# A gated recurrence by products of gates that double with each level, in a two-layer decoder trunk

## The chip, the cores and the metric

The kernel runs on one core of a Trainium2 chip. The metric is the device time of one execution in microseconds (us). The kernel before takes 1434.04 us, the median of three runs (1431.91 to 1434.69). The core has five engines with a queue each, which work in order: TensorE (PE, with its weight loads as PEld), VectorE (DVE), ScalarE (ACT), GpSimd (POOL) and SyncE (SP), which issues the transfers.

## The reference

Two decoder layers on 512 tokens of width 1024. In each, one projection feeds three token mixers side by side, whose outputs are concatenated and projected; then a squared-ReLU feed-forward. The change touches the first mixer (four heads of 64 channels):

```
f = lb + (1.0 - lb) * sigmoid(z);  log_f = log(maximum(f, F_MIN));  k = (1.0 - lb) * sigmoid(-z)
bc = cumsum(log_f)                      # within a chunk
decay[t, s] = exp(bc[t] - bc[s])        # for s <= t, else 0
attn[t, s] = sum_k q[t, k] * decay[t, s, k] * k[s, k]
o = attn @ v + (q * exp(bc)) @ state
state = exp(b_last) * state + (k * exp(b_last - bc))^T @ v
```

The decay depends on the channel, so `attn` is not a single product of two matrices.

## The kernel before, in words

All matrices of the projections are held as a high and a low part, and each product is three matmuls (`mm3`). The tile names in the profile: `whi`, `wlo` are the parts of a weight block `wraw`, `hT` the parts of the transposed activations, `acc` the accumulators; `qrope`, `krope` the queries and keys of the second mixer with RoPE (`ropet` is a scratch tile of it, `qs` the query split in two parts), `aps` its scores; `adaw`, `adaq`, `adacc`, `adas`, `grow` belong to the modulation by `c`; `ang`, `kk`, `rr`, `sin2`, `cos2` to the sine and cosine of the positions, which are computed once, in layer 0.

**The recurrence** works on chunks of 128 tokens, with channels on partitions (two tiles `pr` of 128 channels, that is two heads each, by 512 tokens). `hgq` is the query, `hgk` the key factor, `hgs` the sigmoid of the gate. The generator `recurrence()` forms the gate `ft`, its logarithm `lf` (as a sum of two logarithms, so that very small gates keep their value) and the running sum `hb` by a scan on DVE. The 128x128 triangle of `attn` (`hatt`, one tile per chunk, four heads side by side) is then filled by level. Level `lv` pairs blocks of `h_ = 2**lv` tokens: the later block's queries with the earlier block's keys. With the running sum at the boundary as `mid`, `hx` holds `exp(hb - mid)` in the later half of each pair and `exp(mid - hb)` in the earlier half; the first times `hgq` goes into `hbd`, a block-diagonal tile in which the two heads stand apart, the second times `hgk` stays in `hx`, and one matmul per chunk and `pr` gives the level's scores. A predicated copy by a mask (`lmask`, one plane per level, made at the start) writes them into `hatt`. The diagonal comes first: a product of query and key, summed over channels by matmuls with `heads`, evicted as `hdd`, and spread on `ident`. The levels then run from 6 down to 0. At the end of the mixer `hqe` and `hke` (query and key with their decay over the chunk) and `hebl` carry the state `hst` from chunk to chunk.

**The order** is not the program's own. Every call (`V.`, `A.`, `G.`, `PE.`, `SP.`) is recorded as an operation with its dependences; `vg` and `gv` record two alternatives, DVE or POOL, and `copy` ACT or DVE. A planner, `Plan.schedule`, then places all operations of both layers engine by engine, by rules for cost and by the place in the program, several rounds, and keeps the round that it reckons shortest. So an edit in one place can move instructions anywhere. The recurrence advances one step at each `next(rec, None)`, beside every second step of the projections (`beside`).

Of the kernel before, what the change touches and what calls it, by code (L numbers as in the profile page):

```python
# [684 lines left out]
def trunk(ctx: ExitStack, tc: tile.TileContext, I, out, depth=L):  # L685
# [102 lines left out]
    lmask = static([128, 8, 128], U8, "lmask")  # L788
# [4 lines left out]
    for lv in range(7):  # L793
# [8 lines left out]
    V.tensor_copy(lmask[:, 7, :], ident)  # L802
# [361 lines left out]
    def layer(l, yn, xd, sb1, rest, mods):  # L1164
# [77 lines left out]
        hb = [big(name="hb") for _ in range(2)]  # L1242
        hk = hgk
        one_b = ones[:, 0:1].to_broadcast([128, 128])
        TINY = 2.0 ** -60
# [4 lines left out]
        def recurrence():  # L1250
            for pr in range(2):
                ft, lf = big(name="ft"), big(name="lf")
                V.tensor_scalar(ft, hgs[pr], oml[:, l, pr:pr + 1], lb[:, l, pr:pr + 1], op0=OP.mult, op1=OP.add)
                V.tensor_scalar(hk[pr], hgk[pr], oml[:, l, pr:pr + 1], None, op0=OP.mult)
                V.tensor_scalar(lf, ft, TINY, None, op0=OP.max)
                V.tensor_scalar(ft, ft, 1e-30, 2.0 ** 60, op0=OP.max, op1=OP.mult)
                V.tensor_scalar(ft, ft, 1.0, None, op0=OP.min)
                A.activation(lf, lf, AF.Ln)
                A.activation(ft, ft, AF.Ln)
                vg("tensor_add", lf, lf, ft)  # L1260
                for ch in range(NT):
                    sl = slice(ch * 128, (ch + 1) * 128)
                    V.tensor_tensor_scan(hb[pr][:, sl], one_b, lf[:, sl], 0.0, op0=OP.mult, op1=OP.add)
                yield
# [4 lines left out]
            for lv in (7, 6, 5, 4, 3, 2, 1, 0):  # L1269
                if lv == 7:  # L1270
                    p = ps()[:, :16]
                    for pr in range(2):
                        xd_ = big(name="hx")
                        gv("tensor_mul", xd_, hk[pr], hgq[pr])
                        for ch in range(NT):
                            PE.matmul(p[:, ch * 4 + 2 * pr:ch * 4 + 2 * pr + 2], xd_[:, ch * 128:(ch + 1) * 128], heads,
                                      start=True, stop=True)
                    dd = small([128, 16], "hdd", 2)
                    V.tensor_copy(dd, p)
                    for ch in range(NT):  # L1280
                        gv("tensor_mul", atts[ch], ident[:, None, :].to_broadcast([128, 4, 128]),
                           dd[:, ch * 4:ch * 4 + 4][:, :, None].to_broadcast([128, 4, 128]))
                    yield
                    continue
                h_ = 1 << lv
                nb = 512 // (2 * h_)
                vw = "p (n r h) -> p n r h"
                xf = [None, None]
                for pr in range(2):
                    xf[pr] = big(name="hx")  # L1290
                    bd = diag[lv % 2][pr]
                    bv = hb[pr].rearrange(vw, r=2, h=h_)
                    ev = xf[pr].rearrange(vw, r=2, h=h_)
                    mid = bv[:, :, 0, h_ - 1:h_].to_broadcast([128, nb, h_])
                    vg("tensor_sub", ev[:, :, 1, :], bv[:, :, 1, :], mid)
                    vg("tensor_sub", ev[:, :, 0, :], mid, bv[:, :, 0, :])
                    A.activation(xf[pr], xf[pr], AF.Exp)
                    e5 = xf[pr].rearrange("p (c n r h) -> p c n r h", c=NT, r=2, h=h_)
                    q5 = hgq[pr].rearrange("p (c n r h) -> p c n r h", c=NT, r=2, h=h_)
                    for hh in range(2):  # L1300
                        r_ = slice(hh * 64, hh * 64 + 64)
# [676 lines left out]
```

## Time and profile before

| | before |
|---|---|
| median of 3 runs | 1434.04 us |
| the profiled execution | 1432.88 us |
| its span | 1430.6 us |
| PE busy | 1361.7 us (95%) |
| DVE busy | 1097.3 us (77%) |
| ACT busy | 575.5 us (40%) |
| POOL busy | 489.7 us (34%) |

The span runs from the first to the last instruction on the core; the 2.3 us around it belong to the execution's time. Shares are means over stages that differ: the mixer of layer 0 lies at about 36 to 336 us, the feed-forward of layer 0 to about 748, the mixer of layer 1 at about 752 to 1010, and the rest is the feed-forward of layer 1. A busy PE is not PE at its peak, since matmuls overlap and can run at a lower clock.

### The profile page before, as it was taken

Reading aid. Unit: us, or ns where it says so; the run is one execution under the profiler, and the core shown is the slowest. Engines: PE = TensorE matmul, PEld = TensorE weight load, DVE = VectorE, ACT = ScalarE, POOL = GpSimd, SP = SyncE. Lnnn points to the kernel's source line nnn. Section 1 sums busy time; section 2 is a strip of 40 time slices with the busy share of each in tenths; the row PEclk is TensorE's granted clock in tenths of the full one; section 3 lists DMA queues with packets and bytes.
Section 4 is the critical chain, followed back from the end, with each engine's and each line's share of the span. In section 5 each row is a group of like instructions: output and inputs, shape, how many; then the busy total and the mean of one; then the engine's idle time right before and its main releaser. Section 6 shows DMA issues by size and latency. Waiting matters only on the chain.

```text
span 1430.6 us, 21317 instructions
## 1 busy us (share of the span) xinstructions
PE 1361.7 (95%) x7339; PEld 1135.3 (79%) x7339; DVE 1097.3 (77%) x2305; ACT 575.5 (40%) x1517; POOL 489.7 (34%) x687
## 2 busy tenths in 40 slices
PE   5978999989999999999999989999999999999997
PEld 4766788868888888888889787888888888888886
DVE  8998899988976488385788978899895467634567
ACT  6645387872341223212324455887333112210121
POOL 5678735573310000010223876445721000000023
PEclk9988999998999999999999999999999999999998
DMA  9731554225376276284502334112553234423331
GB/s 305 236 92 29 166 173 146 69 90 163 111 228 212 74 236 204 75 293 155 165 13 83 76 115 145 38 45 89 159 158 103 89 103 139 153 62 104 125 110 59
DMA packets 119843, 185.66 MB, mean 130 GB/s; under 512 B 9796, under 2 KB 47160, under 8 KB 119736
## 3 DMA queue, kind: packets, MB, share of 16 engines
q1 hardware_dynamic: 119736, 184.31, 40.6%
q8 instruction: 58, 0.95, 0.3%
q14 instruction: 49, 0.40, 0.1%
HBM read 175.89 MB, written 8.39 MB: 129 GB/s over the span
## 4 chain that ended last, share of the span: by engine, by line
PE 71%; DVE 16%; ACT 5%; POOL 3%; DMA 2%; issue 2%; SPq 1%; POOLq 0%; DVEq 0%; ACTq 0%
PE acc L681 60%; PE aps L681 6%; PE ps L681 5%; DMA adaq<-in_w_ada_dram 2%; DVE adacc L681 2%; ACT P L681 1%; DVE amax L681 1%; ACT KV L681 1%; DVE PT L681 1%; DVE wlo L681 1%; DVE pcT L681 1%; DVE hb L681 1%; DVE hatt L681 1%; DVE hx L681 1%; DVE rt L681 1%
## 5 line engine op out<-in xcount | busy, mean ns | idle before, releaser
L681 PE MATMUL acc<-hT,whi 128*128 128x512 f32 (+1 forms) x1296 | 413.3, 373 | 4.1 <-ACT hT L681 3.8
L681 POOL TENSOR_TENSOR wlo<-wraw,whi 128x256 fp32r<-128x256 f32 (+2 forms) x122 | 134.9, 1114 | 557.2 <-ACT whi L681 425.4
L681 PE MATMUL acc<-whi,aT 128*128 128x512 f32 x896 | 325.2, 394 | 0.0
L681 PEld LDWEIGHTS acc<-hT,whi 128*128 128x128 f32 x1296 | 234.9, 189 | 49.4 <-ACT hT L681 4.5
L681 PE MATMUL acc<-hT,wlo 128*128 128x512 f32 (+1 forms) x648 | 238.6, 371 | 0.3 <-DVE wlo L681 0.3
L681 PE MATMUL acc<-whi,hT 128*128 128x256 f32 (+2 forms) x1024 | 227.1, 307 | 1.5 <-ACT KV L681 0.9
L681 DVE TENSOR_TENSOR wlo<-wraw,whi 128x512 fp32r<-128x512 f32 (+1 forms) x278 | 193.7, 713 | 11.2 <-ACT whi L681 4.7
L681 PEld LDWEIGHTS acc<-whi,aT 128*128 128x128 f32 x896 | 168.2, 188 | 39.5
L681 ACT ACTIVATE whi<-wraw 128x512 fp32r<-128x512 f32 (+2 forms) x262 | 134.6, 554 | 136.9 <-DMA wraw<-in_w_ff_dram 87.2
L681 ACT ACTIVATE ffa<-acc 128x512 f32<-128x512 f32 x64 | 38.2, 597 | 374.4 <-PE acc L681 373.8
L681 PE MATMUL acc<-wlo,aT 128*128 128x512 f32 x448 | 176.6, 394 | 0.0
L681 PEld LDWEIGHTS acc<-whi,hT 128*128 128x128 f32 x1024 | 168.2, 191 | 8.8 <-issue 1.4
L681 PE MATMUL acc<-wlo,hT 128*128 128x256 f32 (+2 forms) x512 | 157.3, 308 | 0.4 <-DVE wlo L681 0.4
L681 DVE TENSOR_TENSOR ffs<-ffa 128x512 f32<-128x512 f32 x64 | 46.4, 727 | 144.4 <-ACT ffa L681 144.2
L681 PEld LDWEIGHTS acc<-hT,wlo 128*128 128x128 f32 x648 | 122.5, 189 | 23.0 <-DVE wlo L681 0.7
L681 DVE SCALAR_TENSOR_TENSOR adacc<-adaw,silc,adacc 128x512 f32<-128x512 f32 x140 | 110.3, 797 | 12.3 <-DMA adaw<-in_w_ada_dram 10.8
L681 PEld LDWEIGHTS acc<-wlo,hT 128*128 128x128 f32 x512 | 97.6, 191 | 3.4 <-DVE wlo L681 0.6
L681 PEld LDWEIGHTS acc<-wlo,aT 128*128 128x128 f32 x448 | 84.2, 188 | 19.7
L681 ACT ACTIVATE P<-aps,amax 128x128 f32<-128x128 f32 (+3 forms) x128 | 67.8, 535 | 18.0 <-DVE amax L681 16.1
L681 DVE TENSOR_REDUCE amax<-aps 128x1 f32<-128x32 f32 (+4 forms) x192 | 65.6, 380 | 6.1 <-PE aps L681 5.1
L681 POOL TENSOR_SCALAR P<-P,acoef 128x256 f32<-128x256 f32 (+3 forms) x76 | 42.9, 579 | 46.5 <-DVE acoef L681 43.0
L681 DVE CAST whi<-wraw 128x512 fp32r<-128x512 f32 (+1 forms) x138 | 57.0, 415 | 0.3 <-issue 0.2
(327 smaller groups left out, 2453.8 us busy)
## 6 DMA issues: line engine op xcount, KB each, us to landing
wraw<-in_w_ff_dram SPq DMA_DIRECT2D x128, 512.0 KB, 4.6
adaw<-in_w_ada_dram SPq DMA_DIRECT2D x80, 512.0 KB, 4.7
wraw<-in_w_in_dram SPq DMA_DIRECT2D x49, 256.0 KB, 3.6
adaq<-in_w_ada_dram SPq DMA_DIRECT2D x32, 256.0 KB, 6.0
wraw<-in_w_o_dram SPq DMA_DIRECT2D x16, 512.0 KB, 3.8
wraw<-in_w_in_dram SPq DMA_DIRECT2D x15, 512.0 KB, 3.9
xd<-xs SPq DMA_DIRECT2D x24, 256.0 KB, 4.1
xr<-xd SPq DMA_DIRECT2D x24, 256.0 KB, 5.0
```

The costliest lines, as they stand in the source:

```text
L681: getattr(self.handles[e], method)(*a, **k)
```

## The change

The logarithm, the scan, the differences and the exponentials go. `f0` is the gate itself, held at 1e-30 or above. `fts[pr][lv]` holds for each block of `2**lv` tokens the product of its gates; the next level's is the product of neighbours, so it has half as many elements. `fq` and `fk` are the tiles `hgq` and `hgk`, now updated in place: at level `lv` the query has the product of the gates from its block's start to itself, the key the product from behind itself to its block's end. So the later block's queries are only copied into `hbd` (by `copy`, ACT or DVE) and the key tile is the matmul's other operand as it stands. After the copy, the queries of later blocks are multiplied by the earlier block's product; after the matmuls, the keys of earlier blocks by the later block's product. The levels run from 0 up to 6, and after level 6 `fq` and `fk` are what `hqe` and `hke` were, and `fts[pr][7]` replaces `hebl`. The diagonal is spread by ACT in 16 pieces of 128x128 per layer, and levels 5 and 6 are evicted by plain ACT copies of rectangles, so the mask has five planes.

```diff
--- before.py
+++ after.py
@@ -785,12 +785,12 @@
     G.iota(ti, pattern=[[1, 128]], base=0, channel_multiplier=0)
     si = static([128, 1], I32, "si")
     G.iota(si, pattern=[[1, 1]], base=0, channel_multiplier=1)
-    lmask = static([128, 8, 128], U8, "lmask")
+    lmask = static([128, 5, 128], U8, "lmask")
     tsh = big((128, 128), I32, name="tsh")
     tsf = big((128, 128), name="tsf")
     s1 = static([128, 4], I32, "s1")
     sf = static([128, 2], F32, "sf")
-    for lv in range(7):
+    for lv in range(5):
         V.tensor_scalar(tsh, ti, lv, None, op0=OP.logical_shift_right)
         V.tensor_copy(tsf, tsh)
         V.tensor_scalar(s1[:, 0:1], si, lv, None, op0=OP.logical_shift_right)
@@ -799,7 +799,6 @@
         V.scalar_tensor_tensor(sf[:, 0:1], sf[:, 1:2], 1000.0, sf[:, 0:1], op0=OP.mult, op1=OP.add)
         V.tensor_scalar(sf[:, 0:1], sf[:, 0:1], 1.0, None, op0=OP.add)
         V.tensor_scalar(lmask[:, lv, :], tsf, sf[:, 0:1], None, op0=OP.is_equal)
-    V.tensor_copy(lmask[:, 7, :], ident)
...
     inv = static([128, 32], F32, "inv")
@@ -1239,82 +1238,82 @@
...
-        hb = [big(name="hb") for _ in range(2)]
-        hk = hgk
-        one_b = ones[:, 0:1].to_broadcast([128, 128])
-        TINY = 2.0 ** -60
+
+
+
+        fq, fk = hgq, hgk
+        F_MIN = 1e-30
+        fts = [[f] for f in hgs]
+        for f in fts:
+            t, at = big(name="hft"), 0
+            for lv in range(1, 8):
+                f.append(t[:, at:at + (512 >> lv)])
+                at += 512 >> lv
...
         atts = [big((128, 4, 128), name="hatt") for _ in range(NT)]
 
         def recurrence():
+            p = ps()[:, :16]
             for pr in range(2):
-                ft, lf = big(name="ft"), big(name="lf")
-                V.tensor_scalar(ft, hgs[pr], oml[:, l, pr:pr + 1], lb[:, l, pr:pr + 1], op0=OP.mult, op1=OP.add)
-                V.tensor_scalar(hk[pr], hgk[pr], oml[:, l, pr:pr + 1], None, op0=OP.mult)
-                V.tensor_scalar(lf, ft, TINY, None, op0=OP.max)
-                V.tensor_scalar(ft, ft, 1e-30, 2.0 ** 60, op0=OP.max, op1=OP.mult)
-                V.tensor_scalar(ft, ft, 1.0, None, op0=OP.min)
-                A.activation(lf, lf, AF.Ln)
-                A.activation(ft, ft, AF.Ln)
-                vg("tensor_add", lf, lf, ft)
+                f0 = fts[pr][0]
+                V.tensor_scalar(f0, hgs[pr], oml[:, l, pr:pr + 1], lb[:, l, pr:pr + 1], op0=OP.mult, op1=OP.add)
+                V.tensor_scalar(fk[pr], hgk[pr], oml[:, l, pr:pr + 1], None, op0=OP.mult)
+                V.tensor_scalar(f0, f0, F_MIN, None, op0=OP.max)
+                xd_ = big(name="hx")
+                vg("tensor_mul", xd_, fk[pr], fq[pr])
                 for ch in range(NT):
-                    sl = slice(ch * 128, (ch + 1) * 128)
-                    V.tensor_tensor_scan(hb[pr][:, sl], one_b, lf[:, sl], 0.0, op0=OP.mult, op1=OP.add)
+                    PE.matmul(p[:, ch * 4 + 2 * pr:ch * 4 + 2 * pr + 2], xd_[:, ch * 128:(ch + 1) * 128], heads,
+                              start=True, stop=True)
+                vg("tensor_mul", fq[pr], fq[pr], f0)
                 yield
             diag = [[big((128, NT, 2, 64), name="hbd") for _ in range(2)] for _ in range(2)]
             for t in diag[0] + diag[1]:
                 for hh in range(2):
                     G.memset(t[hh * 64:hh * 64 + 64, :, 1 - hh, :], 0.0)
-            for lv in (7, 6, 5, 4, 3, 2, 1, 0):
-                if lv == 7:
-                    p = ps()[:, :16]
-                    for pr in range(2):
-                        xd_ = big(name="hx")
-                        gv("tensor_mul", xd_, hk[pr], hgq[pr])
-                        for ch in range(NT):
-                            PE.matmul(p[:, ch * 4 + 2 * pr:ch * 4 + 2 * pr + 2], xd_[:, ch * 128:(ch + 1) * 128], heads,
-                                      start=True, stop=True)
-                    dd = small([128, 16], "hdd", 2)
-                    V.tensor_copy(dd, p)
-                    for ch in range(NT):
-                        gv("tensor_mul", atts[ch], ident[:, None, :].to_broadcast([128, 4, 128]),
-                           dd[:, ch * 4:ch * 4 + 4][:, :, None].to_broadcast([128, 4, 128]))
-                    yield
-                    continue
+            dd = small([128, 16], "hdd", 2)
+            V.tensor_copy(dd, p)
+            for ch in range(NT):
+                for a in range(4):
+                    A.activation(atts[ch][:, a], ident, AF.Copy, scale=dd[:, ch * 4 + a:ch * 4 + a + 1])
+            yield
+            for lv in range(7):
                 h_ = 1 << lv
-                nb = 512 // (2 * h_)
                 vw = "p (n r h) -> p n r h"
-                xf = [None, None]
                 for pr in range(2):
-                    xf[pr] = big(name="hx")
                     bd = diag[lv % 2][pr]
-                    bv = hb[pr].rearrange(vw, r=2, h=h_)
-                    ev = xf[pr].rearrange(vw, r=2, h=h_)
-                    mid = bv[:, :, 0, h_ - 1:h_].to_broadcast([128, nb, h_])
-                    vg("tensor_sub", ev[:, :, 1, :], bv[:, :, 1, :], mid)
-                    vg("tensor_sub", ev[:, :, 0, :], mid, bv[:, :, 0, :])
-                    A.activation(xf[pr], xf[pr], AF.Exp)
-                    e5 = xf[pr].rearrange("p (c n r h) -> p c n r h", c=NT, r=2, h=h_)
-                    q5 = hgq[pr].rearrange("p (c n r h) -> p c n r h", c=NT, r=2, h=h_)
+                    q5 = fq[pr].rearrange("p (c n r h) -> p c n r h", c=NT, r=2, h=h_)
                     for hh in range(2):
                         r_ = slice(hh * 64, hh * 64 + 64)
-                        vg("tensor_mul", bd[r_, :, hh, :].rearrange("p c (n h) -> p c n h", h=h_), e5[r_, :, :, 1, :],
-                           q5[r_, :, :, 1, :])
-                    vg("tensor_mul", ev[:, :, 0, :], ev[:, :, 0, :], hk[pr].rearrange(vw, r=2, h=h_)[:, :, 0, :])
+                        copy(bd[r_, :, hh, :].rearrange("p c (n h) -> p c n h", h=h_), q5[r_, :, :, 1, :])
+                    tv = fts[pr][lv].rearrange("p (n r) -> p n r", r=2)
+                    qv = fq[pr].rearrange(vw, r=2, h=h_)[:, :, 1, :]
+                    nb = 512 // (2 * h_)
+                    vg("tensor_mul", qv, qv, tv[:, :, 0:1].to_broadcast([128, nb, h_]))
+                    vg("tensor_mul", fts[pr][lv + 1], tv[:, :, 0], tv[:, :, 1])
                 for cp_ in range(2):
                     p = ps().rearrange("p (c m) -> p c m", c=2)
                     for c2 in range(2):
                         ch = 2 * cp_ + c2
                         for pr in range(2):
-                            PE.matmul(p[:, c2, pr * 128:(pr + 1) * 128], xf[pr][:, ch * 128:(ch + 1) * 128],
+                            PE.matmul(p[:, c2, pr * 128:(pr + 1) * 128], fk[pr][:, ch * 128:(ch + 1) * 128],
                                       diag[lv % 2][pr][:, ch].rearrange("p a t -> p (a t)"), start=True, stop=True)
                     for c2 in range(2):
+                        att = atts[2 * cp_ + c2].rearrange("p a (n r h) -> p a n r h", r=2, h=h_)[:, :, :, 1, :]
+                        new = p[:, c2].rearrange("p (a n h) -> p a n h", a=4, h=h_)
+                        if h_ >= 32:
+                            for n in range(64 // h_):
+                                r_ = slice(2 * n * h_, (2 * n + 1) * h_)
+                                A.activation(att[r_, :, n], new[r_, :, n], AF.Copy)
+                            continue
                         V.copy_predicated(
-                            atts[2 * cp_ + c2].rearrange("p a (n r h) -> p a n r h", r=2, h=h_)[:, :, :, 1, :],
-                            lmask[:, lv, :].rearrange("p (n r h) -> p n r h", r=2, h=h_)[:, None, :, 1, :]
-                            .to_broadcast([128, 4, 64 // h_, h_]),
-                            p[:, c2].rearrange("p (a n h) -> p a n h", a=4, h=h_))
+                            att, lmask[:, lv, :].rearrange("p (n r h) -> p n r h", r=2, h=h_)[:, None, :, 1, :]
+                            .to_broadcast([128, 4, 64 // h_, h_]), new)
+                for pr in range(2):
+                    tv = fts[pr][lv].rearrange("p (n r) -> p n r", r=2)
+                    kv = fk[pr].rearrange(vw, r=2, h=h_)[:, :, 0, :]
+                    nb = 512 // (2 * h_)
+                    vg("tensor_mul", kv, kv, tv[:, :, 1:2].to_broadcast([128, nb, h_]))
                 yield
 
         rec = recurrence()
@@ -1627,18 +1626,7 @@
         run(filler)
...
-        qe = [big(name="hqe") for _ in range(2)]
-        ke = [big(name="hke") for _ in range(2)]
-        ebl = small([128, 2, 4], "hebl", 2)
-        for pr in range(2):
-            A.activation(qe[pr], hb[pr], AF.Exp)
-            vg("tensor_mul", qe[pr], qe[pr], hgq[pr])
-            b4 = hb[pr].rearrange("p (n t) -> p n t", t=128)
-            k4 = ke[pr].rearrange("p (n t) -> p n t", t=128)
-            vg("tensor_sub", k4, b4[:, :, 127:128].to_broadcast([128, 4, 128]), b4)
-            A.activation(ke[pr], ke[pr], AF.Exp)
-            vg("tensor_mul", ke[pr], ke[pr], hk[pr])
-            A.activation(ebl[:, pr], b4[:, :, 127], AF.Exp)
+        qe, ke = fq, fk
         for k in range(2):
             mixT[k] = pair(name="mixT")
         st_t = [small([128, 2, 128], "hst", 2) for _ in range(2)]
@@ -1674,7 +1662,7 @@
                         if ch == 0:
                             V.tensor_copy(stn[r_, pr, r_], src)
                         else:
-                            V.scalar_tensor_tensor(stn[r_, pr, r_], sprev[r_, pr, r_], ebl[r_, pr, ch:ch + 1],
+                            V.scalar_tensor_tensor(stn[r_, pr, r_], sprev[r_, pr, r_], fts[pr][7][r_, ch:ch + 1],
                                                    src, op0=OP.mult, op1=OP.add)
             sq = big((128, 256), name="hsq")
             A.activation(sq, po[:, :256], AF.Square)
```

Where the instructions now stand, at three places in layer 0.

PE, before, at the recurrence's first matmuls (`heads` sums the diagonal, `hbd,hx` are levels, `ident,qrope` the transposes of the RoPE queries):

```order
L681 MATMUL acc_1189<-wlo_1178,hT_741 128x512
L681 MATMUL acc_1189<-whi_1169,hT_771 128x512
L681 MATMUL ps_1326<-heads,hx_1225 128x2 x4
L681 MATMUL ps_1326<-heads,hx_1273 128x2 x4
L681 MATMUL ps_1340<-hbd_859,hx_1201 128x128
L681 MATMUL ps_1340<-hbd_862,hx_1216 128x128
L681 MATMUL ps_1348<-ident,qrope_1320 128x128 x2
L681 MATMUL ps_1355<-ident,qrope_1324 128x128 x2
```

PE, now, at level 0:

```order
L681 MATMUL acc_870<-wlo_1032,hT_727 128x256
L681 MATMUL ps_1095<-hbd_848,hgk_975 128x128
L681 MATMUL ps_1095<-hbd_845,hgk_955 128x128
L681 MATMUL ps_1095<-hbd_848,hgk_975 128x128
L681 MATMUL ps_1097<-hbd_848,hgk_975 128x128
L681 MATMUL ps_1097<-hbd_845,hgk_955 128x128
L681 MATMUL ps_1097<-hbd_848,hgk_975 128x128
L681 MATMUL acc_870<-whi_1010,hT_757 128x256
L681 MATMUL acc_882<-whi_1004,hT_716 128x256
```

The first products stood behind 131,596 columns of matmuls, `heads` with them, and beside the RoPE transposes; `heads` now stands behind 83,468 and level 0 behind 91,724, amid the projection, and the first RoPE transpose behind 132,684 instead of 131,916.

DVE, before, between the scans and the sine (`hb` are scans):

```order
L681 TENSOR_TENSOR wlo_1174<-wraw_1068,whi_1163 128x512
L681 SCALAR_TENSOR_TENSOR hb_1153<-ones,lf_1064 128x128
L681 SCALAR_TENSOR_TENSOR rr_1033<-kk_934,rr_1033 128x128
L681 SCALAR_TENSOR_TENSOR hb_1195<-ones,lf_1071 128x128 x4
L681 TENSOR_SCALAR hgk_989<-hgk_989,oml 128x512
L681 SCALAR_TENSOR_TENSOR rr_1033<-kk_934,rr_1033 128x128
L681 TENSOR_SCALAR adacc_1232<-adaw_852,silc 128x512
L681 TENSOR_SCALAR kk_934<-ang_703 128x128
```

DVE, now, before the sine:

```order
L681 COPY_PREDICATED hatt_1158<-lmask,ps_1174 128x128x2
L681 TENSOR_TENSOR hgk_975<-hgk_975,hft_1113 128x128x2
L681 TENSOR_TENSOR wlo_1234<-wraw_1045,whi_1197 128x512
L681 COPY_PREDICATED hatt_1048<-lmask,ps_1229 128x64x4
L681 COPY_PREDICATED hatt_1083<-lmask,ps_1229 128x64x4
L681 COPY_PREDICATED hatt_1141<-lmask,ps_1239 128x64x4
L681 COPY_PREDICATED hatt_1158<-lmask,ps_1239 128x64x4
L681 TENSOR_SCALAR kk_920<-kk_920 128x128
L681 SCALAR_TENSOR_TENSOR rr_1269<-kk_920,ang_695 128x128
```

The scans before the sine are gone, and the predicated copies of levels 0 to 2 (twelve) now stand before it.

ACT, now, at the block copies of levels 0 and 1 (`hbd_845` and `hbd_848` are level 0, `hbd_851` level 1):

```order
L681 ACTIVATE hatt_1048<-ident,hdd_1036 128x128
L681 ACTIVATE whi_1054<-wraw_895 128x256
L681 ACTIVATE hbd_845<-hgq_940 64x4x64 x2
L681 ACTIVATE hatt_1048<-ident,hdd_1036 128x128 x3
L681 ACTIVATE hatt_1083<-ident,hdd_1036 128x128 x2
L681 ACTIVATE whi_1093<-wraw_1017 128x512
L681 ACTIVATE hatt_1083<-ident,hdd_1036 128x128
L681 ACTIVATE hbd_848<-hgq_952 64x4x64 x2
L681 ACTIVATE hbd_851<-hgq_940 64x4x64 x2
```

Where ACT had logarithms and exponentials with table loads between them, it now has block copies with diagonal pieces between them.

## Rows read from the trace of the kernel before

**Rows 1.** The page: engines over the span; the granted clock in 40 slices (tenths).

```profile
PE 1361.7 (95%) x7339; PEld 1135.3 (79%) x7339; DVE 1097.3 (77%) x2305; ACT 575.5 (40%) x1517; POOL 489.7 (34%) x687
PEclk9988999998999999999999999999999999999998
```

**Rows 2.** Busy by stage: stretch, length, engines busy (instructions), granted clock, DMA share, GB/s.

```profile
36.00:92.00 56.00, 52.59 (x316) 46.18 (x314) 53.87 (x104) 31.52 (x57) 36.13 (x42) 0.97 0.64 190
92.00:121.00 29.00, 14.45 (x67) 11.83 (x67) 26.50 (x63) 10.26 (x21) 26.12 (x33) 0.61 0.17 52
121.00:180.00 59.00, 54.04 (x335) 43.52 (x334) 51.38 (x134) 28.93 (x97) 47.23 (x71) 0.99 0.38 117
288.00:336.00 48.00, 42.98 (x236) 34.62 (x235) 40.64 (x89) 29.29 (x80) 32.78 (x44) 0.89 0.31 99
752.00:868.00 116.00, 107.19 (x735) 96.23 (x735) 98.15 (x229) 54.05 (x148) 81.18 (x108) 0.99 0.32 91
```

**Rows 3.** Timeline of PE from 90 us: start, length, instruction, count [idle before <-releaser].

```profile
90.18 0.64 PE L681 MATMUL acc<-whi,hT 128*128 128x512 f32 x2
...
90.89 0.62 PE L681 MATMUL acc<-whi,hT 128*128 128x512 f32 x2
...
91.80 2.01 PE L681 MATMUL ps<-heads,hx 128*128 128x2 f32 x16
102.93 1.19 PE L681 MATMUL ps<-hbd,hx 128*128 128x128 f32 x4 [9.12 <-DVE qrope L681]
...
112.31 3.57 PE L681 MATMUL ps<-hbd,hx 128*128 128x128 f32 x16 [2.38 <-DVE qs L681]
...
120.37 0.77 PE L681 MATMUL acc<-whi,hT 128*128 128x512 f32 x1
...
131.39 1.50 PE L681 MATMUL ps<-hbd,hx 128*128 128x128 f32 x12
```

**Rows 4.** Timeline of DVE from 69 us.

```profile
69.92 0.16 DVE L681 TENSOR_SCALAR oml<-lb 128x4 f32<-128x4 f32 x1
...
78.48 2.10 DVE L681 TENSOR_TENSOR_SCAN hb<-ones,lf 128x128 f32<-128x128 f32 x3 [1.19 <-POOL lf L681]
...
98.35 0.63 DVE L681 TENSOR_SCALAR sin<-sin 128x128 f32<-128x128 f32 x1
...
102.38 1.07 DVE L681 TENSOR_TENSOR qrope<-acc,cos 128x256 f32<-128x256 f32 x3
```

**Rows 5.** Groups of POOL, whole span: count | busy us, mean ns | idle before.

```profile
L681 POOL TENSOR_TENSOR hbd<-hx,hgq 64x256 f32<-64x256 f32 x39 | 32.8, 843 | 9.1 <-ACT hx L681 6.4 <-issue 1.1
L681 POOL TENSOR_TENSOR hx<-hb 128x256 f32<-128x256 f32 x47 | 32.4, 705 | 4.6 <-issue 2.6 <-DVE hb L681 1.5
```

**Rows 6.** Groups of DVE, whole span.

```profile
L681 DVE COPY_PREDICATED hatt<-lmask,ps 128x256 f32<-128x256 uint8 x56 | 25.5, 526 | 3.8 <-PE ps L681 3.5
...
L681 DVE SCALAR_TENSOR_TENSOR qs<-ps,qs 64x256 fp32r<-64x256 f32 x32 | 12.9, 421 | 1.3 <-ACT qs L681 0.4
...
L681 DVE CAST whi<-wraw 128x256 fp32r<-128x256 f32 x22 | 7.4, 340 | 0.3 <-issue 0.2
...
L681 DVE SCALAR_TENSOR_TENSOR rr<-kk,rr 128x128 f32<-128x128 f32 x4 | 2.4, 608 | 0.0
```

**Rows 7.** The tile hx on DVE: minimum/median/maximum ns, first and last start.

```profile
L681 DVE TENSOR_TENSOR hx<-hx,hgk x16: 409/840/2043, 123.1 to 861.4; 128x256 f32<-128x256 f32 x16
```

**Rows 8.** Groups of ACT, whole span.

```profile
L681 ACT ACTIVATE whi<-wraw 128x256 fp32r<-128x256 f32 x74 | 28.1, 415 | 10.9 <-PE acc L681 7.9 <-DMA wraw<-in_w_in_dram 1.4 <-PE aps L681 1.4
...
L681 ACT ACTIVATE hx<-hx 128x512 f32<-128x512 f32 x28 | 17.4, 628 | 22.6 <-POOL hx L681 12.6 <-DVE hx L681 9.8
...
L681 ACT ACT_TABLE_LOAD x12 | 15.4, 1283 | 1.0 <-PEq L1966 0.8
...
L681 ACT ACTIVATE adat<-adaq,silc 128x128 f32<-128x128 f32 x14 | 4.5, 388 | 1.1 <-DMA adaq<-in_w_ada_dram 1.1
```

**Rows 9.** Who waited for whom, 750 to 870 us: total, times, longest.

```profile
PE ps L681 <- DVE hx L681: 4.8, 4, 2.3
```

## The prediction

> **What bounds the kernel now.** I read the first part of the page, then a table by stage, then the timelines of the stages in which TensorE (PE) stands still. PE is busy 95% of the span and its clock is down in two short places [rows 1], so only some 69 us of the span are not matmuls. By stage [rows 2]: the feed-forward stages have no idle PE to give back. The mixer of layer 0 has it: from 92 to 121 us PE is busy 14.45 of 29.00 us at a granted clock of 0.61, that is mostly at the lower of its levels (1.2 of 2.4 GHz), while VectorE (DVE) is busy 26.50 and GpSimd (POOL) 26.12. The 67 instructions there would take 67 x 0.125 = 8.4 us at the pace that the same matmuls have later (12 in 1.50 us) [rows 3], so this place loses 20.6 us. From 121 to 180 another 5.0 us are idle, from 288 to 336 5.0 us, and in the mixer of layer 1 (752 to 868) 8.8 us.
>
> Why 92 to 121 is empty: at 91.80 PE starts the recurrence's `heads` products, and its next instruction is a recurrence product at 102.93, after 9.12 us of waiting, followed by sparse ones at half pace (16 in 3.57 us at 112.31); the dense projection goes on at 120.37 [rows 3]. Those products and the RoPE transposes beside them wait for DVE. DVE has `oml` at 69.92, goes through the gate, its logarithm and its scans (78.48), and only at 98.35 finishes the sine that RoPE needs; the RoPE products stand at 102.38 [rows 4]. So layer 0 waits for a queue of DVE and POOL work, of which the recurrence is the largest part.
>
> **The change part by part**, both layers together, prices from rows, counts from the rows and from the new order.
>
> POOL loses 39 `hbd` products (32.8 us) and 47 subtractions (32.4 us) [rows 5]; of the new products of 256 elements 38 stand on POOL, 38 x 0.69 = 26 us. Net about -39 us, before the eight diagonal products that go to ScalarE.
>
> DVE loses 42 operations of that size (17 `hbd`, 16 and 9 `hx`), at the median of 840 ns of one of the three groups [rows 7] 35 us; 16 scans at 0.70 us (three in 2.10) [rows 4], 11 us; 16 of 56 predicated copies at 25.5/56 = 0.455 us [rows 6], 7 us. It gains 18 products of 256 elements, 18 x 0.84 = 15 us. Net about -38 us.
>
> ScalarE (ACT) loses 28 exponentials (17.4 us) and five of twelve table loads (5 x 1.28 = 6.4 us) [rows 8]. It gains 51 of 56 block copies. No row shows such a copy of 64 partitions x 256 strided elements; it lies between 0.388 (128x128 with a scale pointer) and 0.62 us (the 128x512 exponential), and a loss or gain by the stride cannot be excluded. I take the 415 ns of 128x256, which has its number of elements [rows 8]: 51 x 0.415 = 21 us. The 32 diagonal pieces have the form of the 388 ns row, 12 us; 24 evictions of the last two levels add some 7 us at 0.3 each, an estimate from the same row. Net about +9 us on an engine that is busy 54 of 116 us in layer 1's stage and 10 of 29 in the gap [rows 2]: it costs nothing unless the queue of ACT becomes the late one, which is weighed below.
>
> The multiplications with a broadcast operand have the shape of the subtractions with the broadcast middle that they replace, so their price is bounded by the 409 and 2043 ns of one row [rows 7]; at 2043 they would eat half of the gain, at 409 add to it.
>
> **What that makes of the gap.** PE reaches the old `heads` at 91.8; the new order puts them 48,000 columns earlier and three levels of products among the projection, while the first RoPE transpose stays where it was in columns. The pace is 512 columns in 0.237 us (three in 0.71, from 90.18 to 90.89) [rows 3], 2.16 a ns. I follow the new queues by hand. From `oml` at 70 DVE needs some 4.7 us for the scaled gates and the first decayed query (eight operations at 0.4 to 0.8): 74.7. ACT then copies half the blocks, does six diagonal pieces and a weight cast, and copies the other half: 5 us, 79.7. PE comes to level 0 39,900 columns, 18.4 us, before the 91.8, plus 2.0 for the 16 `heads` and 1.3 for the projection between the halves: 76.7, so it waits 3 us. Each next level is a loop: eight products, predicated copies of 0.455, an update of 0.84, four copies of 0.415; PE reaches level 1 at 83 and goes at 85, level 2 at 88.3 and goes at 90. DVE has four predicated copies of level 2 behind that (92), then eleven operations at about 0.6 (`rr`, 608 ns [rows 6]): the sine stands at 98.6, as before, and the RoPE products at 102. Up to there nothing is won on DVE, but PE comes to the first transpose at 90 + 1 + 25,600/2160 = 103, with 24 recurrence products done (3.0 us), where before it stood idle. From there DVE has 16 query splits at 0.421 [rows 6], 6.7 us, and the rope products, 14 us in all; PE has 20,000 columns, 9.2 us, and 24 short products. So the key stage's first transpose starts at about 116, where before it stood behind the twelve products of 131.39 [rows 3], at 132.7. Gain 16.
>
> Where ACT's copy costs 0.62 the three levels are 2.5 us later and the gain is 13.5. What is late next is DVE's sine, behind 12 predicated copies.
>
> Other terms: in 121 to 180, -2 of the 5.0 idle us, since DVE and POOL have some 14 us less to do there; 288 to 336 keeps its chain (its operations are not touched), 0; layer 1, where PE waited 4.8 us for `hx` [rows 9], -3 of 8.8; two mask levels fewer at the start, where DVE waits for transfers, 0. Sum -21. The profiled execution took 1432.88 us (span 1430.6 and 2.3 around it): 1411.9. The median of the runs is 1.2 us above it: 1413.
>
> A rule that speaks against the copies on ACT: "ScalarE: Activation LUTs", section "Rules for kernel authors", of the Trainium skill puts additions and multiplications on VectorE and not on ScalarE. The rows agree in the price, 340 ns for DVE's cast of 128x256 against ACT's 415 [rows 6, 8]; by that rule DVE would do the 51 copies in 17 us and its net gain would shrink from 38 to 21 us, so the rule leaves out which engine is short here.
>
> **The rivals.**
> A, the gap only moves. DVE stands in order, and 12 predicated copies that wait for PE now lie before the sine. If each of the three levels is 3 us later than I reckon, the sine is at 107 and PE waits again, at the lower clock. Gain 7 in the gap, 1 and 1 elsewhere: 1425. For it: ACT holds 16 diagonal pieces (6.2 us) among the first block copies. Against: DVE has 9 us of logarithms and scans less before it.
> B, more than the gap. DVE's 256-element operation takes 409 ns at best and 840 in the median [rows 7]; where POOL works less, the same operations on DVE end sooner. All of 20.6 + 5.0 + 8.8 us comes back: 1434 - 34 = 1400. Against: some handoffs stay. "VectorE Performance Modes" in "Advanced Engine Details and Errata" of the Trainium skill says that GpSimd and VectorE share a port and block each other; this is the mechanism of B, and by it alone the rest of DVE's work would also gain.
> C, slower. All 14 levels become one chain through three engines, as queries and keys are now updated in place: a level's products wait for the copies of the decayed query, its key update for the products. PE takes its queue in order, so each late level holds the projection behind it. At 2.5 us a level (four copies 1.7, one update 0.84) PE would lose 35 us against 21 won: 1448. From 1.5 us a level on the sign turns. Against: outside of the first three levels of layer 0 the new order leaves PE 8,000 columns and more, 4 us, between levels.
> D, nothing: the freed engines are filled with other work that was waiting anyway, and PE's waits stay: 1434.
>
> **How the numbers follow.** Forecast 0.55, A 0.17, B 0.18, C 0.07, D 0.03. The likeliest case gives 1413; its own range is 1405 to 1421 (copy price, one or two levels late). 1399 to 1430 takes in A and B and leaves out C, D and the tails. The runs tell no change from 0.2%, 2.9 us. Faster 0.89, same 0.04, slower 0.07.
>
> **What would show it.** Right: `heads` before 75 us, no wait over 5 us of PE between 85 and 120, the granted clock of 92 to 121 at 0.9 or more, the key stage's transposes near 116, POOL's busy time down by 40 us or more. Wrong: a sine after 105 with PE idle before it (A); PE waits of 2 us and more before most of the 14 levels (C); ACT's block copies far from 0.4 us.

## The result: 1399.2 us, 34 us faster, and where they came from

The changed kernel takes 1399.2 us (median of 4 runs, 1397.67 to 1401.03), the kernel before in the same session 1433.38 (1431.91 to 1434.69): a ratio of 0.9762, 95% interval 0.9745 to 0.9779. The forecast of 1413 named the right direction and the right first place, but its gain of 21 us was too small by 13; the number is that of rival B (1400).

The page of the profile after, the line of the engines and that of the clock, beside [rows 1]:

```profile
PE 1346.9 (96%) x7339; PEld 1124.7 (81%) x7339; DVE 1051.6 (75%) x2242; ACT 580.2 (42%) x1570; POOL 428.5 (31%) x623
PEclk9999999999999999999999999999999999999999
```

The span fell from 1430.6 to 1396.5. TensorE's idle time fell from 68.9 us (1430.6 - 1361.7) to 49.6, that is 19.3; its busy time fell by 14.8 with the same instructions, since they ran at a mean granted clock of 0.993 in place of 0.981. So nearly half of the gain is pace, which stands in no wait. VectorE lost 45.7 us of work and GpSimd 61.2; ScalarE gained 4.7.

The table by stage, the first three stretches of [rows 2] at the same microseconds, then layer 1's stretch, taken 26 us earlier:

```profile
36.00:92.00 56.00, 53.31 (x346) 47.69 (x345) 52.84 (x94) 35.39 (x80) 44.43 (x58) 0.97 0.63 186
92.00:121.00 29.00, 26.75 (x147) 21.60 (x146) 27.20 (x87) 19.70 (x60) 20.54 (x33) 1.00 0.24 67
121.00:180.00 59.00, 54.23 (x375) 45.46 (x373) 43.84 (x143) 35.52 (x145) 24.59 (x45) 0.97 0.61 188
726.00:842.00 116.00, 113.50 (x780) 100.13 (x779) 89.40 (x255) 60.51 (x183) 52.59 (x81) 1.00 0.42 123
```

The gap is closed: 147 matmuls where there were 67, at a granted clock of 1.00, the upper level. Layer 1's stretch has 2.5 idle us where it had 8.8, with GpSimd at 52.59 in place of 81.18.

A stretch at fixed microseconds holds other work after a change. The total of columns that TensorE moves is the same in both traces (7339 matmuls, 2,686,260 columns), so I added them up instruction by instruction and read when the matmul starts with which the same amount is reached. Inside a mixer the two orders differ, and marks next to each other scatter by 2 us; in the feed-forward they scatter by 0.3.

| columns done | where | before | after | difference |
|---|---|---|---|---|
| 80,000 | start over | 68.3 | 67.5 | -0.8 |
| 160,000 | behind the gap | 134.3 | 114.0 | -20.3 |
| 240,000 | early attention, layer 0 | 193.6 | 174.3 | -19.3 |
| 440,000 | late attention, layer 0 | 309.9 | 289.2 | -20.7 |
| 480,000 | output projection, layer 0 | 342.4 | 319.8 | -22.6 |
| 600,000 | feed-forward, layer 0 | 399.8 | 376.4 | -23.4 |
| 1,360,000 | layer 1 begins | 746.6 | 723.5 | -23.1 |
| 1,600,000 | its recurrence done | 894.7 | 862.7 | -32.0 |
| 2,600,000 | end | 1381.1 | 1347.5 | -33.6 |

Two tiles say the same in rows: the output projection's first and last start and the feed-forward's, before and then after (count: minimum/median/maximum ns, first to last start; forms).

```profile
L681 PE MATMUL acc<-whi,mixT x128: 387/393/793, 301.0 to 1037.7; 128*128 128x512 f32 x128
L681 ACT ACTIVATE ffa<-acc x64: 579/598/602, 409.9 to 1375.9; 128x512 f32<-128x512 f32 x64
```

```profile
L681 PE MATMUL acc<-whi,mixT x128: 387/394/628, 279.7 to 1003.7; 128*128 128x512 f32 x128
L681 ACT ACTIVATE ffa<-acc x64: 577/598/603, 386.7 to 1342.4; 128x512 f32<-128x512 f32 x64
```

Layer 0's first output product is 21.3 us earlier, the first feed-forward tile 23.2, layer 1's last output product 34.0. So about 23 us come from layer 0 and 10 to 11 from layer 1; the feed-forward of layer 0 gave nothing (-23.4 at 600,000 columns, -23.1 where layer 1 begins).

The timeline of TensorE after, answering to [rows 3]:

```profile
69.19 1.05 PE L681 MATMUL ps<-heads,hx 128*128 128x2 f32 x8
...
74.85 0.60 PE L681 MATMUL ps<-hbd,hgk 128*128 128x128 f32 x4
...
85.76 1.80 PE L681 MATMUL ps<-hbd,hgk 128*128 128x128 f32 x14 [0.83 <-DVE hgk L681]
...
109.75 2.02 PE L681 MATMUL ps<-hbd,hgk 128*128 128x128 f32 x16 [1.64 <-DVE qs L681]
...
112.08 0.38 PE L681 MATMUL ps<-ident,krope 128*128 128x128 f32 x2
...
124.84 0.51 PE L681 MATMUL acc<-whi,hT 128*128 128x280 f32 x1 [2.29 <-ACT KV L681]
```

and that of VectorE, to [rows 4]:

```profile
65.22 0.92 DVE L681 TENSOR_SCALAR oml<-lb 128x4 f32<-128x4 f32 x1
...
94.68 0.22 DVE L681 TENSOR_SCALAR sin<-sin 128x128 f32<-128x128 f32 x1
...
97.01 1.40 DVE L681 TENSOR_TENSOR qrope<-acc,cos 128x256 f32<-128x256 f32 x4
```

In place of the wait of 9.12 us stand waits of 0.83, 1.64 and 2.29. The last of them was 0.93 before: it is ScalarE's queue of key evictions, now with block copies between them.

### The profile page after: what moved, and what is told of

It reads as the page before. It is cut to its first block, busy times and chain, and to the rows that moved or that the text cites. A ratio compares the mean times of both kernels' runs of the same rounds, so it can differ in the third digit from the quotient of the medians.

```text
span 1396.5 us, 21252 instructions
## 1 busy us (share of the span) xinstructions
PE 1346.9 (96%) x7339; PEld 1124.7 (81%) x7339; DVE 1051.6 (75%) x2242; ACT 580.2 (42%) x1570; POOL 428.5 (31%) x623
## 4 chain that ended last, share of the span: by engine, by line
PE 75%; DVE 12%; ACT 4%; DMA 4%; issue 2%; POOL 2%; SPq 1%; POOLq 0%; DVEq 0%; ACTq 0%
PE acc L681 64%; PE aps L681 7%; PE ps L681 5%; DMA adaw<-in_w_ada_dram 2%; DVE adacc L681 1%; DMA adaq<-in_w_ada_dram 1%; DVE amax L681 1%; DMA wraw<-in_w_in_dram 1%; DVE ge L681 1%; ACT P L681 1%; ACT KV L681 1%; DVE PT L681 1%; SPq L681 1%; DVE r L681 1%; DVE rt L681 1%
## 5 line engine op out<-in xcount | busy, mean ns | idle before, releaser
L681 POOL TENSOR_TENSOR wlo<-wraw,whi 128x256 fp32r<-128x256 f32 (+2 forms) x133 | 152.6, 1158 | 612.9 <-ACT whi L681 533.3
L681 PE MATMUL acc<-whi,hT 128*128 128x256 f32 (+2 forms) x1024 | 230.2, 308 | 3.3 <-ACT KV L681 2.5
L681 DVE TENSOR_TENSOR wlo<-wraw,whi 128x512 fp32r<-128x512 f32 (+2 forms) x267 | 182.7, 700 | 13.6 <-ACT whi L681 6.4
L681 ACT ACTIVATE whi<-wraw 128x512 fp32r<-128x512 f32 (+2 forms) x253 | 131.3, 556 | 120.1 <-DMA wraw<-in_w_ff_dram 71.8
L681 DVE SCALAR_TENSOR_TENSOR adacc<-adaw,silc,adacc 128x512 f32<-128x512 f32 x140 | 113.8, 823 | 15.4 <-DMA adaw<-in_w_ada_dram 13.8
L681 ACT ACTIVATE P<-aps,amax 128x128 f32<-128x128 f32 (+3 forms) x128 | 66.9, 530 | 14.3 <-DVE amax L681 12.2
L681 PE MATMUL aps<-PT,Vt 128*128 128x512 f32 x160 | 51.4, 414 | 3.8 <-DVE PT L681 3.1
```

What stands on the lines that cost most here:

```text
L681: getattr(self.handles[e], method)(*a, **k)
```

## The experiments

Two theories. Load: the gain is the work taken off VectorE and GpSimd, wherever they are a queue that TensorE waits for. Chain: it is the shorter chain (no logarithm, scan, exponential) and the earlier start. Every edit makes the planner write a new order, unless the text says that the order was kept. Each time is a median over timed rounds beside the kernel before (1433.3 to 1434.7 in the three sessions).

**Load put back, order made anew.**

```
+ for _ in range(2 - hh):                    # 84 in all, overwritten by the copy
+     vg("tensor_mul", bd[...], f5[r_, :, :, 0, :], f5[r_, :, :, 1, :])
  copy(bd[...], q5[...])
```

> The changed kernel plus 84 products of 64 partitions x 256 elements that compute nothing that is used: each block half gets one or two products of gates before the copy overwrites it, as many as the change took away net, on VectorE or GpSimd. They need no query, so they lengthen no chain of the recurrence; they only fill the two engines (84 x about 0.8 = 67 us). Load theory: the 34 us came from work taken off VectorE and GpSimd, so most of them go again: 1420 to 1432, and the median of the two-engine products goes back from 0.43 to 0.8 us. Chain theory: they came from the shorter chain (no logarithm, scan, exponential) and the earlier start of the recurrence, and the load is beside: 1399 to 1406.

1441.68 us, ratio to before 1.0054 (1.0039 to 1.0069): over the top of the load theory's range. But it does not decide. The row of its `heads` products:

```profile
L681 PE MATMUL ps<-heads,hx x32: 167/251/338, 97.8 to 780.6; 128*128 128x2 f32 x32
```

The planner counted the new work and began the recurrence at 97.8 in place of 69.2. Load and start moved together, so later runs keep the order. A late start alone does not cost that: the fastest order below (1395 us) begins the recurrence at 98.6.

```profile
L681 PE MATMUL ps<-heads,hx x32: 167/251/251, 98.6 to 744.7; 128*128 128x2 f32 x32
```

**The change in two parts.** The algebra alone, with the diagonal on GpSimd or VectorE and the last two levels as predicated copies (the edit in short):

```
- A.activation(atts[ch][:, a], ident, AF.Copy, scale=dd[...])      # x32
+ gv("tensor_mul", atts[ch], ident[...], dd[...])                  # x8
- if h_ >= 32: ... A.activation(att[...], new[...], AF.Copy)
```

> The changed kernel with the diagonal again a product on GpSimd or VectorE (8 of about 1.14 us) and the last two levels again predicated copies on VectorE (16 of 0.44 us, seven mask planes); only the products of gates and the block copies on ScalarE are left of the change. Load theory: 16 us of about 100 come back onto the two engines, so about 5 us of 34 go: 1404. Chain theory: nothing, 1399 to 1401. If ScalarE is the late queue between 116 and 125 us (24 key evictions with block copies between them, TensorE waits 2.3 us there), the 19 us less on ScalarE give up to 2 us: 1397.

1400.65 us, ratio 0.9775 (0.9758 to 0.9792). And the reverse, these two moves alone in the kernel before:

> The kernel before with only the diagonal (32 pieces) and the evictions of the last two levels (24) moved to ScalarE and five mask planes; logarithms, scans, differences, exponentials and block products as before. Load theory: 16 us less on VectorE and GpSimd, about 5 us faster: 1428. Chain theory: no change, 1433; with the products of gates alone together (1399 to 1401) this makes the whole.

1435.44 us, ratio 1.0006 (0.9992 to 1.0019). The moves to ScalarE give nothing that can be measured; the products of gates are the change. Both times lie by the numbers of the chain theory (1399 to 1401, and 1433), and the load theory's 1404 and 1428 did not come. As another order alone moves the time by up to 7 us (below), two runs with new orders can't settle a difference of 5.

**Block copies on VectorE.** `copy(bd[...])` becomes `V.tensor_copy(bd[...])`.

> The changed kernel with all 56 block copies on VectorE: ScalarE loses 51 x 0.417 = 21 us, VectorE gains 51 x 0.285 = 15 us. Load theory: 15 us more of VectorE's work cost about 5 us: 1404. Chain theory: a level becomes shorter by 0.13 us a copy and one handoff, and nothing was late: 1399. Late ScalarE: the wait of 2.3 us for the key evictions near 122 us goes: 1397.

1407.40 us, ratio 0.9816 (0.9799 to 0.9832): 8 us slower than the change, where the load theory had 5. As orders alone differ by nearly as much (below), this is no more than a hint.

**Load put back, order kept.** The order of the changed kernel is left as it is, and when it is written out, one product on constants stands beside each block copy, on VectorE, on GpSimd, or on both (the edit in short):

```
  if method in ("activation", "tensor_copy") and out is "hbd":      # 56 places
+     vector.tensor_mul(ones[0:64], ident2, ident2)     # 64x256, read by nothing
+     gpsimd.tensor_mul(ones[64:128], ident2, ident2)
```

> The changed kernel with every instruction in its place, and beside each of the 56 block copies one more product of 64x256 on VectorE and one on GpSimd, on constants, which nothing reads (56 x 0.58 = 32 and 56 x 0.73 = 41 us by the rows of the run with 84 such products, about what the change took off each engine). Load theory: the time goes back by 20 to 30 us, to 1420 to 1430. Chain theory: the order and the shorter chain are as in the changed kernel, so 1399 to 1406. Place theory (the load counted in the run with 84 products because the order was made anew and the recurrence put later): also under 1406.

> As the run with both, with the 56 products on GpSimd alone (41 us). Load theory with collisions: GpSimd's work lengthens VectorE's two-operand instructions, so about half of the loss of both: 1408 to 1416. If only VectorE's own queue counts: 1399 to 1403.

> As the run with both, with the 56 products on VectorE alone (32 us). If VectorE's queue is what TensorE waits for: nearly all of the loss of both, 1412 to 1425. Load theory with collisions: half of it, 1408 to 1416. Chain theory: 1399 to 1403.

The same on ScalarE, as a copy:

> The changed kernel with every instruction in its place and one more copy of 64x256 on ScalarE ahead of each of the 56 block copies (56 x 0.42 = 23 us), which nothing reads. If ScalarE has room, as the prediction had it (580 us busy of 1397): 1399 to 1404. If any engine in the level's chain counts like VectorE and GpSimd, where a us of work cost 0.68 and 0.73 us: 23 x 0.7 = 16 us, 1415.

| added to the changed kernel | its work | median us | added time | us per us |
|---|---|---|---|---|
| VectorE and GpSimd | 36.3 + 42.3 | 1434.80 (1.0010, 0.9996 to 1.0024) | 35.6 | 0.45 |
| GpSimd | 37.0 | 1426.12 (0.9949, 0.9934 to 0.9963) | 26.9 | 0.73 |
| VectorE | 31.1 | 1420.36 (0.9904, 0.9889 to 0.9918) | 21.2 | 0.68 |
| ScalarE | 56 x 0.402 = 22.5 | 1410.70 (0.9834, 0.9804 to 0.9864) | 11.5 | 0.51 |

With 78.6 us of load back and every instruction in its place, the time is that of the kernel before; the chain theory allowed 1406. So TensorE's time does follow these queues. That it is just the time of the kernel before is in part chance: the change took off 106.9 us (45.7 + 61.2), and counted by columns the loaded run is 1.6 us earlier than the kernel before at 160,000 columns, 2.7 earlier where layer 1 begins, and 5.8 later at 1,600,000. In layer 0 the load takes away most of the gain, in layer 1 more than all of it. GpSimd's load alone cost more than either theory had expected (1408 to 1416, or 1399 to 1403). That the parts add to more than both (48 against 36) fits with waits that hide behind each other; no run takes them apart. ScalarE is not free either, against what the prediction had; its four runs are far apart (1406.96 to 1415.41).

Who waits, in the run with GpSimd's products alone: the waits of TensorE over the whole span (total, times, longest), the added products, and the page's engines.

```profile
PE ps L686 <- POOL qrope L686: 11.8, 4, 5.7
PE ps L686 <- POOL adacc L686: 5.8, 1, 5.8
PE ps L686 <- POOL krope L686: 5.0, 5, 1.9
PE ps L686 <- POOL hgk L686: 4.5, 1, 4.5
```

```profile
L685 POOL TENSOR_TENSOR ones<-ident x56: 610/612/947, 73.6 to 837.1; 64x256 bf16<-64x256 f32 x56
```

```profile
PE 1354.9 (95%) x7339; PEld 1130.1 (79%) x7339; DVE 1060.2 (74%) x2242; ACT 580.2 (41%) x1570; POOL 465.4 (33%) x679
```

In the changed kernel the wait for `adacc` was 5.7 already and that for `qrope` 0.8; the rest, some 20 us, is new. How it comes is seen in the timelines of that run, first TensorE's, then ScalarE's:

```profile
86.98 2.93 PE L686 MATMUL ps<-hbd,hgk 128*128 128x128 f32 x12 [4.50 <-POOL hgk L686]
...
110.56 0.69 PE L686 MATMUL ps<-ident,qrope 128*128 128x128 f32 x2 [4.28 <-POOL qrope L686]
```

```profile
91.52 0.86 ACT L686 ACTIVATE hbd<-hgq 64x256 f32<-64x256 f32 x2 [5.77 <-POOL hgq L686]
...
102.26 0.86 ACT L686 ACTIVATE hbd<-hgq 64x256 f32<-64x256 f32 x2 [5.25 <-POOL hgq L686]
...
105.48 0.31 ACT L686 ACTIVATE sin<-rr 128x128 f32<-128x128 f32 x1
```

GpSimd's queries and keys come late, TensorE waits for one, ScalarE's block copies for the other; the sine stands behind those copies and runs at 105.5, in the changed kernel at 94.1, and RoPE waits for it. So here a queue that is late passes its lateness on through the engines that stand in order behind it, and an engine that is busy 33% of the span can be the one that counts. This is rival A, made by hand. The collisions of rival B are there, but small: VectorE's own instructions, the same 2242 in the same order, take 8.6 us longer (1060.2 against 1051.6). The Trainium skill ("Advanced Engine Details and Errata", "VectorE Performance Modes") says that GpSimd and VectorE's two-port instructions block each other; here VectorE's five block copies go from a median of 285 to 654 ns, which agrees. Products of two operands slow down as well: VectorE's added ones have a median of 454 ns when it has them alone and of 646 with GpSimd's beside them.

**Other orders of the same instructions.** Only the recurrence's place in the plan moves: -40, -160 and 0 in place of -100.

```
- RSHIFT = -100
+ RSHIFT = -40        # and -160, and 0
```

> The changed kernel with the recurrence's place in the plan moved by 60 places (RSHIFT -40 in place of -100) and nothing else: how far the time moves when the planner only makes another order of the same instructions. If the orders are equivalent: within 4 us of 1399. If the gain rests on this one order: 1410 and more.

> The changed kernel with the recurrence planned 60 places earlier (RSHIFT -160), nothing else: a second measure of how far another order of the same instructions moves the time. Scatter of the planner: 1395 to 1406. If an earlier recurrence is what gives the gain, it is faster than 1399; if the later one at -40 (1395) points the way, slower than 1399.

> As the run before, with the recurrence planned 100 places later (RSHIFT 0). Scatter: 1395 to 1406. If later is better: under 1395.

1395.07 (1394.11 to 1396.09; ratio 0.9730, 0.9716 to 0.9745), 1405.75 (0.9797, 0.9780 to 0.9814) and 1397.91 (0.9747, 0.9731 to 0.9763). All keep most of the gain. In each, the planner also chose anew which engine does what. The four orders spread over 11 us, and earlier is not better. A difference of 5 us between two kernels of different order says little about an edit. Nor do the sums of load set the time: the slowest of the four, at -160, has GpSimd busy 66.9 us less than the change and VectorE, with 81 instructions more, only 2.9 more.

```profile
PE 1351.0 (96%) x7339; PEld 1128.1 (80%) x7339; DVE 1054.5 (75%) x2323; ACT 581.2 (41%) x1564; POOL 361.6 (26%) x550
```

**A candidate.** On top of -40, the diagonal and the last evictions may go to VectorE too (the edit in short):

```
- A.activation(atts[ch][:, a], ident, AF.Copy, scale=d1)
+ plan.op([("A", "activation", ...), ("V", "tensor_scalar", ...)])   # ScalarE or VectorE
- A.activation(att[...], new[...], AF.Copy)
+ copy(att[...], new[...])                     # ScalarE or VectorE
```

> A candidate: the order with RSHIFT -40, and the 32 diagonal pieces and the 24 evictions of the last two levels may go to ScalarE or VectorE as the planner chooses, in place of ScalarE alone. If ScalarE near the key evictions is what is still late (a wait of 2.3 us in the changed kernel): 1391 to 1395. If VectorE's work counts at 0.68 us a us and ScalarE's at nothing, the pieces that go over cost: 1395 to 1401.

1395.18 us (1393.36 to 1397.11), ratio 0.9720 (0.9703 to 0.9737): no better than -40 alone. That order, at 1395, is the fastest found, 4 us under the change, and its runs don't overlap with the change's.

## Why the prediction was right in its place and short in its size

**The gap** was the right place, and its markers came: `heads` at 69.2 (under 75), no wait over 5 us between 85 and 120, a clock of 1.00 from 92 to 121, the key stage's transposes at 112.1 (forecast 116), GpSimd down by 61.2 us (40 or more). At equal work it gave 19 to 20 us (from -0.8 to -20.3) where 16 were forecast. The step that was mis-sized is the waits of 3, 2 and 1.7 us before the first three levels: only one of 0.83 us came. I kept `oml` at its old 69.9, but the new order has it at 65.2, so the chain behind it stood earlier, and the sine was ready at 94.7 in place of 98.6.

**121 to 180** was to give 2 and gave back 1.0 (from -20.3 to -19.3): TensorE waits 2.29 us there for the key evictions, which share ScalarE with the block copies. This is the late queue that the prediction weighed in the gap, where it did not come.

**288 to 336** was put at nothing, "its operations are not touched". That was a misreading: `qe, ke = fq, fk` takes the last exponentials and products out of it. It gave 1.9 (from -20.7 at 440,000 columns to -22.6). What differs in the rows is the clock: its lower level holds for 10 us before, and for 3.4 after, just ahead of the first products with the state:

```profile
324.00:334.00 10.00, 9.74 (x38) 8.38 (x38) 7.21 (x17) 3.69 (x10) 6.01 (x9) 0.50 0.34 105
```

```profile
299.00:302.50 3.50, 3.26 (x9) 2.18 (x9) 3.28 (x9) 1.70 (x6) 3.38 (x3) 0.51 0.99 358
```

Why is open: the run with both loads back gains as much there (from -1.1 to -3.0), so the load is not shown to be the cause; the run with only the moves to ScalarE, which keeps these operations, gains 0.7 in another order, which does not decide for the operations.

**Layer 1** is the term that failed: -3 forecast, about -10 measured. I credited a part of the 4.8 us that TensorE waited for `hx` [rows 9], by name. The rest of its 8.8 idle us were waits for other tiles, of ScalarE and GpSimd, and most of them went as well. The waits of 750 to 870 us before that I left out, then those of 726 to 842 us after, of which these are the longest:

```profile
PE ps L681 <- ACT krope L681: 2.0, 2, 1.1
PE ps L681 <- POOL qrope L681: 1.2, 1, 1.2
```

```profile
PE ps L681 <- POOL qrope L681: 0.8, 1, 0.8
PE ps L681 <- ACT krope L681: 0.5, 1, 0.5
PE ps L681 <- DVE chid L681: 0.4, 1, 0.4
```

Idle time makes 6.3 of the ten (8.8 to 2.5). The forecast priced no clock in this layer: before, the granted clock stood at its lower level for 10.2 us with TensorE full, an estimated 5.1 us at half the pace; after, it is 1.00 from 303 to 1390 us. Part of that is lost again, since TensorE is idle for 5.8 us behind 1,600,000 columns where it was 2.8. The rows of the clock before:

```profile
846.00:849.40 3.40, 3.40 (x17) 3.40 (x16) 1.48 (x5) 1.29 (x4) 1.97 (x2) 0.50 0.52 162
1006.50:1013.30 6.80, 6.80 (x25) 5.97 (x25) 3.90 (x11) 3.38 (x8) 6.47 (x9) 0.50 0.25 78
```

**The prices** were mostly right. ScalarE's tiles, and the new products of both engines:

```profile
L681 ACT ACTIVATE hbd<-hgq x51: 401/417/444, 72.6 to 811.7; 64x256 f32<-64x256 f32 x51
L681 ACT ACTIVATE hatt<-ident,hdd x32: 385/387/403, 71.8 to 755.2; 128x128 f32<-128x128 f32 x32
L681 POOL TENSOR_TENSOR hgq<-hgq,hft x18: 612/696/1068, 82.6 to 809.2; 128x256 f32<-128x256 f32 x18
L681 POOL TENSOR_TENSOR hgk<-hgk,hft x15: 627/672/1063, 83.3 to 828.0; 128x256 f32<-128x256 f32 x15
L681 DVE TENSOR_TENSOR hgk<-hgk,hft x9: 406/425/818, 85.0 to 828.0; 128x256 f32<-128x256 f32 x9
L681 DVE TENSOR_TENSOR hgq<-hgq,hft x6: 403/456/792, 77.7 to 812.1; 128x256 f32<-128x256 f32 x6
```

Block copy 417 ns (415 taken), diagonal piece 387 (388), GpSimd's product 0.70 and 0.67 us (0.69); only VectorE's product took half of the 0.84 that I read from a crowded median. GpSimd's -39 us came out at -61: I left out its smaller groups, the twelve `hx` products (9.4 us), the tail's `hqe` and `hke` (13.2) and `lf` (5.6), besides the diagonal (9.4), and against them the planner gave it 17.7 us more of the weight splits `wlo`, of which VectorE lost 11.0. ScalarE's +9 was added up wrongly: the terms as written (21 + 12 + 7 - 17.4 - 6.4) make +16. It came out at +4.7, since the logarithms (5.0) and the exponentials of the tail (5.7) went too.

**What was missing** is the step from these sums to time. My -38 and -39 us were worth 21 in the forecast because they counted only where a wait of the recurrence stood in the trace. Putting 78.6 us back, at 56 places, costs 35.6: at that price, 0.45 us per us, the forecast's own sums would have given 35, near the 34 measured. That they meet is in part luck, for the 106.9 us that really went would have given 48. The price is one of these 56 places, ahead of the updates in the level's chain; load put elsewhere was not tried, and how much of the 34 us the shorter chain gave by itself stays open. Rival B had the size, since it let all idle time come back, but not the cause: added up by the mean of each tile and shape, the 2143 instructions that VectorE has in both kernels take the same time in both, within 0.1 us. Nor did all of its sum come: the 5.0 us of 121 to 180 stayed (4.8 after). The measured time lies at the very edge of 1399 to 1430, a range that reached so low only to take in B. Rivals A, C and D did not come: the sine was ready, and between 60 and 330 us TensorE waited 0.8 us for a tile of the recurrence (`hgk`).

## What to carry to other kernels

Where two helper engines are busy through a stage in which TensorE has gaps, price the work that a change takes off them by the queue and not only by the waits that carry the removed tile's name: whatever stands behind in the same queue moves up too. To measure that price, keep the order and add work that nobody reads, and take it for the places where it was added; in this kernel a new order of the same instructions moved the time by 1 to 7 us for that alone. Compare stages at equal work done and not at equal microseconds.

## What the runs showed that was not expected

Short idle places can cost more than their length. Before the change TensorE is full from 324 to 334 us, 9.74 of 10, at a granted clock of 0.50, the lower of its levels, right behind this wait (the timeline of the kernel before):

```profile
321.99 0.68 PE L681 MATMUL ps<-hst,hqe 128*128 128x128 f32 x4 [1.56 <-DVE hst L681]
```

They need not: the run with both loads back is idle for 7.27 us between 288 and 336, more than the 5.0 of the kernel before, at a clock of 1.00.

```profile
288.00:336.00 48.00, 40.73 (x240) 31.86 (x240) 44.22 (x99) 31.94 (x83) 34.80 (x46) 1.00 0.30 100
```

And runs of one kernel in one order spread with the clock: the four with ScalarE's copies took 1406.96, 1407.70, 1413.70 and 1415.41 us at mean clocks of 0.994, 0.991, 0.987 and 0.985. Which of the two follows the other, these numbers do not tell.
